# Prompt keys and queries stored once and split in the attention stage

## The chip, the cores and the metric

The kernel runs on one core of one Trainium2 chip. The metric is the device time of one launch in microseconds, the median of three runs. TensorE (PE) multiplies matrices, VectorE (DVE), ScalarE (ACT) and GpSimd (POOL) work on tiles element by element, and SyncE (SP) issues most of the transfers between DRAM and SBUF; PSUM is the memory that PE writes its results to. Times in the profile are counted from the first instruction.

## The reference: what is computed

One inference step of a hybrid decoder with two layers, for a new prompt (1 x 2048 tokens) and, at once, for 8 sequences that each add 8 tokens to 4096 cached ones. D is 1024, with 16 heads of 64.

```python
# layer 1, recurrent (RG-LRU)
z = rms_norm(x) @ w_in; u, g = split(z)
u = causal_conv(u); h = scan(gates(u))
x = x + rms_norm((h * silu(g)) @ w_out)
# keys, values and log forget values, made once
k, v, f = split(rms_norm(x, kv_norm) @ w_kv);  c = cumsum(log_sigmoid(f + b_f))
# layer 2, forgetting attention
q, g = split(rms_norm(x) @ b_w_in)
s = q k^T / 8 + c_query - c_key, causal;  p = softmax(s);  o = p v
y = x + rms_norm((o * silu(g)) @ b_w_out)
```

The outputs are y, the new keys, values and log forget values of prompt and samples, and the recurrent states. Everything is float32. The samples attend to their cached pages, which a page table points to.

## The kernel before, in words

**Precision.** Most products are made in a faster matrix format that keeps fewer bits (F32R). An operand x is split into a high part h, x rounded to that format, and a low part l = x - h, and a product is h·h + h·l + l·h. `evac_pair` (line 361) makes such a pair from PSUM: ACT copies (rounding), DVE subtracts.

**Stages.** The prompt goes through in chunks: the recurrent layer for the first 1024 tokens and the samples, then the projections (`phase_b`, line 859) of keys, values, queries and gates for them; then the recurrent layer for the other 1024, and the projections for these in two chunks of 512 (about 1240 to 1700 us of the profile). `B_ORDER` (line 45) sets the order of the column blocks. In `token_major` (line 885) keys and values come out with a token per partition, go to the outputs, and the values also to a DRAM copy `v_d` (line 915). `keys` (line 871) transposes the keys on PE, splits them with `evac_pair` and writes both parts to `kd_d` (lines 882, 883), which holds a low and a high row for each feature. `feature_major` (line 925) makes queries with a feature per partition, splits them (lines 940, 941) and writes both parts to `qd_d` (lines 943, 944).

**Decode.** `decode` (line 1013) computes attention over the cache for 16 turns (8 sequences, 2 groups of 8 heads). Each turn loads its 32 pages of keys and of values in groups of four (`raw`, line 1074, four buffers), transposes the keys on DVE (line 1159), multiplies on PE (lines 1127 and 1237) and makes a softmax with a block of eight exponentials on ACT (line 1196). Two turns run beside the first projections; the other 14 beside the later projections and the prompt attention.

**Prompt attention** (`attention`, line 1290, about 1700 to 2890 us). A unit is a head and a block of 512 queries; the 64 units run over the heads, 0,1,2,3 and 3,2,1,0 in turn. A head has 40 ticks, one for each block of 128 keys of each of its units. In a tick PE makes the scores `st` (keys by queries) with two matmuls (lines 1537 and 1538), and a third on the diagonal (line 1540) for the mask; ACT makes `p` = exp(st) (line 1546); every four ticks PE multiplies p with the values (`ops`, line 1557); POOL adds up p for the sums (line 106, the helper `tt`). There are two PSUM banks for `st`, so PE can be two ticks ahead of ACT. The row maxima are found first: `top` (line 1394) makes scores `sx` with high parts only (line 1404), DVE reduces them (lines 1406, 1408), and ACT writes the negative maximum into four rows of the query tile (line 1423). `advance` (line 1502) issues these `LEAD` = 18 ticks ahead.

The operands are tiles of 128 rows. `kbt` and `qbt` hold the high part in rows 0 to 63 and, below, the rows for c, the maximum and ones; `ka` holds low and high keys and `qa` high and low queries, so that line 1537 gives both cross products in one pass. `load_keys` (line 1368) fills kbt from the high rows, `load_head` (line 1375) fills ka (both parts) and the values `vvt` from `v_d`, `load_unit` (line 1383) fills qbt and `load_low` (line 1388) qa. A head's keys are loaded at the first tick of the head before, ka and the values three ticks later; a unit's queries one and two units ahead. Before the first unit the loads stand on ACT's queue, then on SP's.

**Order.** The program is written as interleaved generators: `Side.along` (line 1009) runs the decode beside the attention in proportion to estimated costs, and `Later` (line 339) delays steps by ticks. A scheduling pass then sets the order of instructions on each engine, and each engine and each queue works strictly in that order. An SP transfer that waits for a free buffer holds those behind it.

## Time and profile before

| What | Value |
|---|---|
| Median of three runs | 3090.09 us |
| The three runs | 3083.68, 3090.09 and 3090.77 us |
| Span of the profiled execution, first to last instruction | 3081.2 us |
| Time of the profiled execution around its span | not on the page; the median is 8.9 us above the span |
| Granted PE clock, mean of the span | 0.965 |
| Moved by DMA | 653.25 MB, mean 212 GB/s |

How to read it: the page gives the busy time of each engine, and views of the trace give the same for stretches of time (windows), for groups of instructions by line, for waits (who waited for whom: total us, times, longest us), and the chain of waits that leads back from the last instruction. A name like qbt<-qd is what an instruction writes and reads. PEld is PE's loading of weights, SPq and ACTq are transfers issued on those queues. "DMA share" is the mean busy share of the 16 DMA engines and "PEclk" the part of PE's full clock that was granted.

### The profile page before, as it was taken

The page shows a single profiled execution, that of the slowest core. Times are in us where ns is not written, and L with a number is a line of the kernel's source. Part 1 is how long each engine was busy: PE and PEld are TensorE (multiplying, and loading weights), DVE is VectorE, ACT ScalarE, POOL GpSimd, SP SyncE. Part 2 cuts the span into 40 slices and gives each one's busy share as a digit, 9 for nine tenths or more (in the row PEclk, how much of TensorE's full clock was granted, in tenths as well). Part 3 has the DMA queues.
Part 4 walks back from the last instruction along what each step waited for, and adds up shares of the span by engine and source line. Part 5 has one row for each costly group of instructions (what it writes and reads, how often), then busy time and mean ns, then how long its engine had stood idle before and what let it go on. Part 6 is the DMA issues. An engine that isn't in the chain of part 4 may idle for free.

```text
span 3081.2 us, 58151 instructions
## 1 busy us (share of the span) xinstructions
PE 2825.8 (92%) x20462; PEld 2177.5 (71%) x20462; DVE 1805.6 (59%) x4012; ACT 1295.0 (42%) x2874; POOL 1155.5 (38%) x1263
## 2 busy tenths in 40 slices
PE   6998999998999989997999799899999988999798
PEld 5997888988999978885797455455545554544587
DVE  7876555424367756755655666666667665543244
ACT  4665432232346655333333334444444445455211
POOL 1663101000025532000001456655656648788322
PEclk9999999999999999998999799999999999999899
DMA  4224547788622266999999998989999996331343
GB/s 121 89 76 150 154 137 216 242 267 254 198 84 86 79 195 198 327 305 315 325 331 307 292 303 261 289 268 321 289 294 314 317 295 211 97 87 41 96 135 111
DMA packets 492855, 653.25 MB, mean 212 GB/s; under 512 B 91100, under 2 KB 292829, under 8 KB 485286
## 3 DMA queue, kind: packets, MB, share of 16 engines
q1 hardware_dynamic: 488934, 643.87, 66.9%
q10 hardware_dynamic: 3340, 3.56, 0.4%
q8 instruction: 162, 2.65, 0.4%
q0 software_dynamic: 288, 2.10, 0.2%
q14 instruction: 131, 1.07, 0.1%
HBM read 513.82 MB, written 135.16 MB: 211 GB/s over the span
## 4 chain that ended last, share of the span: by engine, by line
PE 54%; DMA 20%; DVE 10%; ACT 5%; SPq 5%; issue 4%; POOL 2%; ACTq 0%; DVEq 0%; POOLq 0%
PE ops L1557 5%; DMA raw<-in_cache_k_dram 5%; PE y L368 4%; PE y L370 4%; PE y L369 4%; PE st L1537 3%; DMA raw<-in_cache_v_dram 3%; PE kv L369 3%; PE kv L368 3%; PE kv L370 3%; PE sx L1404 3%; PE dO L1237 2%; SPq L1074 2%; PE qg L368 2%; PE st L1538 2%
## 5 line engine op out<-in xcount | busy, mean ns | idle before, releaser
L106 POOL TENSOR_TENSOR acc<-acc,p 128x512 f32<-128x512 f32 (+3 forms) x576 | 638.8, 1109 | 291.7 <-PE ops L1557 226.4
L1546 ACT ACTIVATE p<-st 128x512 f32<-128x512 f32 (+3 forms) x576 | 290.4, 525 | 404.8 <-PE st L1538 188.6
L1159 DVE STREAM_TRANSPOSE ktr<-raw 128x1024 f32<-128x1024 f32 x256 | 305.4, 1223 | 161.3 <-DMA raw<-in_cache_k_dram 143.7
L1406 DVE TENSOR_REDUCE mxs<-sx 128x1 f32<-128x512 f32 x384 | 253.9, 680 | 143.5 <-PE sx L1404 142.5
L369 PE MATMUL kv<-wl,xh 128*128 128x256 f32 (+3 forms) x1088 | 309.1, 287 | 8.9 <-DVE wl L413 8.8
L368 PE MATMUL kv<-wh,xh 128*128 128x256 f32 (+3 forms) x1088 | 310.4, 290 | 5.7 <-ACT wh L412 5.3
L370 PE MATMUL kv<-wh,xl 128*128 128x256 f32 (+3 forms) x1088 | 309.2, 286 | 0.0
L1557 PE MATMUL ops<-p,vvt 128*64 128x512 f32 (+3 forms) x1152 | 292.7, 550 | 3.1 <-ACT p L1546 2.8
L1537 PE MATMUL st<-qa,ka 128*128 128x512 f32 (+3 forms) x640 | 273.3, 427 | 21.8 <-ACT p L1546 18.0
L1404 PE MATMUL sx<-kbt,qbt 96*128 96x512 f32 (+3 forms) x640 | 234.7, 426 | 26.1 <-DMA qbt<-qd 11.5
L1537 PEld LDWEIGHTS st<-qa,ka 128*128 128x128 f32 x640 | 123.6, 193 | 178.5 <-issue 112.1
L412 ACT ACTIVATE wh<-wst,gv 128x256 fp32r<-128x256 f32 (+1 forms) x384 | 164.4, 499 | 195.0 <-DMA wst<-in_b_w_in_dram 81.8
L1538 PE MATMUL st<-qbt,kbt 128*128 128x512 f32 (+3 forms) x640 | 237.0, 371 | 0.0
L413 DVE SCALAR_TENSOR_TENSOR wl<-wst,gv,wh 128x256 fp32r<-128x256 f32 (+1 forms) x384 | 169.9, 492 | 108.1 <-ACT wh L412 100.3
L368 PE MATMUL qg<-xh,wh 128*128 128x384 f32 (+2 forms) x640 | 229.1, 359 | 1.0 <-ACT wh L412 1.0
L370 PE MATMUL qg<-xh,wl 128*128 128x384 f32 (+2 forms) x640 | 227.5, 357 | 0.9 <-DVE wl L413 0.9
L369 PE MATMUL qg<-xl,wh 128*128 128x512 f32 (+2 forms) x640 | 226.9, 356 | 0.0
L1092 POOL TENSOR_TENSOR qw<-qb,amask 128x128 f32<-128x128 f32 x64 | 29.3, 465 | 498.8 <-PE dS L1127 258.0
L369 PEld LDWEIGHTS kv<-wl,xh 128*128 128x128 f32 (+1 forms) x1088 | 203.8, 188 | 12.7 <-DVE wl L413 10.4
L368 PEld LDWEIGHTS kv<-wh,xh 128*128 128x128 f32 (+1 forms) x1088 | 203.6, 189 | 11.8 <-ACT wh L412 6.0
L370 PEld LDWEIGHTS kv<-wh,xl 128*128 128x128 f32 (+1 forms) x1088 | 205.3, 189 | 3.9 <-issue 3.9
L1404 PEld LDWEIGHTS sx<-kbt,qbt 96*128 96x128 f32 x640 | 119.1, 203 | 94.4 <-DVE mxs L1406 25.1
(289 smaller groups left out, 6472.1 us busy)
## 6 DMA issues: line engine op xcount, KB each, us to landing
raw<-in_cache_k_dram SPq DMA_DIRECT2D x512, 256.0 KB
raw<-in_cache_v_dram SPq DMA_DIRECT2D x512, 256.0 KB
wst<-in_w_kv_dram SPq DMA_DIRECT2D x48, 512.0 KB
wst<-in_b_w_in_dram SPq DMA_DIRECT2D x48, 512.0 KB
xt<-in_x_prompt_dram SPq DMA_DIRECT2D x32, 512.0 KB
wst<-in_a_w_in_dram SPq DMA_DIRECT2D x64, 256.0 KB
x<-x SPq DMA_DIRECT2D x32, 512.0 KB
out_dram<-kf SPq DMA_DIRECT2D x128, 128.0 KB
```

The source lines that it names most:

```text
L106: eng.tensor_tensor(out, a, b, op=op)
L368: T.matmul(ps, lh(k), rh(k), start=(k == 0), stop=False)
L369: T.matmul(ps, lh(k), rl(k), start=False, stop=False)
L370: T.matmul(ps, ll(k), rh(k), start=False, stop=(k == nk - 1))
L413: V.scalar_tensor_tensor(wl[:, k, :], st[:, k, :], gk, f(wh[:, k, :]), op0=ALU.mult, op1=ALU.subtract)
L1159: V.transpose(t.kts[pp][:, n], raw[:, :, pp * 256:(pp + 1) * 256])
L1404: T.matmul(ps[:, :w], qb[0:96, j * P:(j + 1) * P], kb[0:96, ck * 512:ck * 512 + w], start=True, stop=True)
L1406: V.reduce_max(mx[:, j, ck:ck + 1], ps[:, :w], axis=AX.X)
L1537: T.matmul(ps[:, lo:], ka[:, ks], qa[:, lo:], start=True, stop=False)
L1538: T.matmul(ps[:, lo:], kb[:, ks], qb[:, lo:], start=False, stop=(k < qc * 4))
L1546: pair.append((k, lo, p, A.activation(p[:, lo:], ps[:, lo:], AF.Exp)))
L1557: return T.matmul(ops[r:r + HD, lo:], vvs[h % 2][:, k, :], p[:, lo:], start=(k < 2), stop=(last and k >= todo[-1][0] - 1))
```

## The change

`kd_d` and `qd_d` hold each key and query once, in float32. In the projections, ACT copies keys and queries from PSUM to one tile, which is written; DVE's subtractions there and the second writes go. The DRAM copy of the values goes too; the attention reads values from the output.

In the attention, a head's keys are loaded once, into rows 0 to 63 of ka. `split_keys` then makes both parts for each of four chunks of 512 keys, at ticks 10 to 13 of the head before: ACT copies with rounding into kbt and into rows 64 to 127 of ka, and DVE subtracts in place for the low part. A unit's queries are loaded once, into rows 0 to 63 of qa; `split_unit` copies on ACT to qbt, subtracts on DVE into rows 64 to 127, and copies in place on ACT to round. Loads are issued one unit earlier than before (`bring`), and a unit is split five ticks after its load, or when it is needed (`part`). qa has six buffers in place of four. To make room, tiles of the recurrent layer move to a pool that is closed before the attention, and the tiles `cs` and `odd` share one buffer.

```diff
-    kd_d, qd_d = dt_("kd", [D, 2, SEQ]), dt_("qd", [D, 2, SEQ])
+    kd_d, qd_d = dt_("kd", [D, SEQ]), dt_("qd", [D, SEQ])
-    v_d = dt_("vd", [SEQ, D])
...
-                evac_pair(th[:, :w], tl[:, :w], ps[:, :w])
+                A.copy(tf[:, :w], ps[:, :w])
-                S.dma_start(kd_d[r0:r0 + P, 1, tk:tk + w], f(th[:, :w]))
-                S.dma_start(kd_d[r0:r0 + P, 0, tk:tk + w], f(tl[:, :w]))
+                S.dma_start(kd_d[r0:r0 + P, tk:tk + w], tf[:, :w])
...
-                        S.dma_start(v_d[tok:tok + m, sl], kf[:m, :])
...
-                            A.mul(th[:, :nn], ps[:, :nn], 0.125)
-                            V.scalar_tensor_tensor(tl[:, :nn], ps[:, :nn], 0.125, f(th[:, :nn]),
-                                                   op0=ALU.mult, op1=ALU.subtract)
-                            S.dma_start(qd_d[r * P:(r + 1) * P, 0, pt:pt + w], f(th[:, so:nn]))
-                            S.dma_start(qd_d[r * P:(r + 1) * P, 1, pt:pt + w], f(tl[:, so:nn]))
+                            A.mul(tf[:, :nn], ps[:, :nn], 0.125)
+                            S.dma_start(qd_d[r * P:(r + 1) * P, pt:pt + w], tf[:, so:nn])
...
         def load_keys(h):
-                queue[0].dma_start(f(kb[0:64, lo:hi]), kd_d[h * HD:(h + 1) * HD, 1, lo:hi])
+                queue[0].dma_start(f(ka[0:64, lo:hi]), kd_d[h * HD:(h + 1) * HD, lo:hi])
                 queue[0].dma_start(f(kb[64:67, lo:hi]), nc_d[h, :, lo:hi])
+        def split_keys(h, c):
+            ka, kb = heads[h], kbs[h % 2]
+            sl = slice(c * 512, (c + 1) * 512)
+            A.copy(kb[0:64, sl], f(ka[0:64, sl]))
+            A.copy(ka[64:P, sl], f(ka[0:64, sl]))
+            tt(V, ka[0:64, sl], f(ka[0:64, sl]), f(kb[0:64, sl]), ALU.subtract)
+            loaded.add((h, c))
...
-            queue[0].dma_start(f(qbs[u % NQ][0:64, :]), qd_d[h * HD:(h + 1) * HD, 0, qc * 512:(qc + 1) * 512])
-        def load_low(u):
...
+            qa = qas[u] = pool.tile([P, 512], F32R, name="qa", tag="qa", bufs=NQ)
+            queue[0].dma_start(f(qa[0:64, :]), qd_d[h * HD:(h + 1) * HD, qc * 512:(qc + 1) * 512])
+        def split_unit(u):
+            qa, qb = qas[u], qbs[u % NQ]
+            A.copy(qb[0:64, :], f(qa[0:64, :]))
+            tt(V, qa[64:P, :], f(qa[0:64, :]), f(qb[0:64, :]), ALU.subtract)
+            A.copy(qa[0:64, :], f(qa[0:64, :]))
...
+        def bring(u, tick):
+            while done[1] <= min(u, len(units) - 1):
+                load_unit(done[1])
+                since[done[1]] = tick
+                done[1] += 1
...
+            if done[0] < len(tasks):
+                bring(min(tasks[done[0]][0] + 2, done[2] + NQ - 1), tick)
+            if done[3] < done[1] and since[done[3]] + 5 <= tick:
+                part(done[3])
...
+                if 10 <= at < 14 and h + 1 < H:
+                    split_keys(h + 1, at - 10)
```

More of the change, by code (lines that the diff above doesn't have):

```diff
@@ L221, in tile_hawk_fox, with kt_ @@
     small = ctx.enter_context(tc.tile_pool(name="small", bufs=4))
+    wkeep = ExitStack()
+    wkept = sbuf(wkeep, "slots")
+    def kt_(name, shape):
+        return wkept.tile(shape, F32, name=name, tag=name)
+    gv = kt_("gv", [P, KB, 43])
+    hb_ga, hb_gx = kt_("hb_ga", [P, KB]), kt_("hb_gx", [P, KB])
+    nsp4, psp4 = kt_("nsp4", [P, KB]), kt_("psp4", [P, KB])
+    bfB = kt_("bfB", [P, H])
+    halo = kt_("halo", [P, KB, 3])
+    G.memset(halo[:, :, :], 0.0)
+    hcar = kt_("hcar", [P, KB])
+    G.memset(hcar[:, :], 0.0)
+    ccar = kt_("ccar", [H, 1])
+    G.memset(ccar[:, :], 0.0)
+    st_s = kt_("st_s", [P, KB, 32])
+    st_p = kt_("st_p", [P, KB, 4])
     def rsqrt(ss, m, scale, post=None, w=1):
@@ L1317, in attention @@
         pool.tile([P, 512], F32, name="oT", tag="oT", bufs=5)
-        pool.tile([P, 512], F32, name="cs", tag="cs")
+        pool.tile([P, 512], F32, name="odd", tag="odd")
         pool.tile([P, 512], F32, name="sgt", tag="sgt", bufs=2)
@@ L1460, in total @@
                 T.matmul(ps[qc * 32:(qc + 1) * 32, :], ones[:, :32], acc[:, :], start=True, stop=True)
-            cs = pool.tile([P, 512], F32, name="cs", tag="cs")
+            cs = pool.tile([P, 512], F32, name="cs", tag="odd")
             rows = slice(0, P) if len(todo) == 4 else slice(qc * 32, (qc + 1) * 32)
@@ L1499, in attention, with part @@
         start = [sum(nks[:u]) for u in range(len(units))]
-        done = [0, 0, 0]
+        done = [0, 0, 0, 0]
+        since = {}
+        def bring(u, tick):
[3 more added lines that the diff above has]
+                done[1] += 1
+        def part(u):
+            while done[3] <= u:
+                split_unit(done[3])
+                done[3] += 1
         def advance(tick):
@@ L1510, in advance @@
                 u, j, ck = tasks[done[0]]
-                while done[1] <= min(u + 1, len(units) - 1):
-                    load_unit(done[1])
-                    done[1] += 1
+                bring(u + 1, tick)
+                part(u)
                 top(u, j, ck)
                 done[0] += 1
+            if done[0] < len(tasks):
+                bring(min(tasks[done[0]][0] + 2, done[2] + NQ - 1), tick)
+            if done[3] < done[1] and since[done[3]] + 5 <= tick:
+                part(done[3])
         load_keys(0)
         tick = 0
+        split_keys(0, 0)
+        split_keys(0, 1)
         advance(-1)
-        load_head(0)
-        load_low(0)
-        load_low(1)
+        load_values(0)
+        split_keys(0, 2)
+        split_keys(0, 3)
         queue[0] = S
```

46 lines of the change are left out of this document (11 added, 35 removed).

## The prediction

> **What bounds the kernel now.** The page first: it has the span, and which engine is near its limit.
>
> ```profile
> span 3081.2 us, 58151 instructions
> PE 2825.8 (92%) x20462; PEld 2177.5 (71%) x20462; DVE 1805.6 (59%) x4012; ACT 1295.0 (42%) x2874; POOL 1155.5 (38%) x1263
> ```
>
> TensorE (PE) is busy 92% of the span. An average over stages says little, so the second view is the windows over the stretches that the change touches: the second pass of the projections (1240 to 1700 us), the start of the prompt attention, the attention with the decode beside it, the attention alone, and, for comparison, the projections' first pass.
>
> ```profile
> core 0: us, PE busy (x) PEld busy (x) DVE busy (x) ACT busy (x) POOL busy (x), PEclk, DMA share, GB/s
> 1240.00:1700.00 460.00, 430.07 (x3936) 368.47 (x3938) 271.06 (x524) 159.15 (x409) 20.09 (x35) 0.96 0.98 319
> 1700.00:1740.00 40.00, 23.12 (x148) 14.02 (x140) 21.20 (x49) 6.60 (x17) 11.28 (x17) 0.61 1.04 303
> 1740.00:2560.00 820.00, 751.09 (x6624) 427.81 (x6622) 554.24 (x1131) 360.75 (x877) 507.76 (x490) 0.96 0.94 294
> 2560.00:2890.00 330.00, 300.47 (x1346) 158.04 (x1342) 149.55 (x346) 169.94 (x358) 259.36 (x227) 0.98 0.34 93
> ...
> 400.00:870.00 470.00, 448.39 (x3805) 431.82 (x3806) 211.49 (x442) 137.04 (x349) 16.87 (x44) 0.99 0.71 220
> ```
>
> Here the DMA engines are as full as PE: 0.98 and 0.94 of the time from 1240 to 2560 us. PE is idle 460 - 430.07 = 29.9 us in the projections, 820 - 751.09 = 68.9 us beside the decode, 29.5 us in the attention alone. The third view is the chain of waits, for the projections and for the attention beside the decode:
>
> ```profile
> by line: DMA raw<-in_cache_k_dram 12.7%; PE kv L369 7.4%; PE kv L368 7.3%; PE kv L370 7.2%; DMA wst<-in_w_kv_dram 6.2%; DMA sgd<-tgb 5.7%; DMA sc<-cd 4.7%; SPq L1074 4.5%; issue 3.8%; PE dS L1127 3.6%; DVE wl L413 3.6%; PE qg L368 3.5%; DMA
> by line: PE ops L1557 11.3%; DMA raw<-in_cache_k_dram 10.2%; DMA raw<-in_cache_v_dram 8.5%; PE st L1537 7.4%; PE dO L1237 6.6%; PE sx L1404 6.3%; SPq L1074 5.6%; PE dS L1127 5.1%; issue 4.9%; PE st L1538 4.9%; DMA sc<-cd 4.8%; DVE ktr L1159
> ```
>
> Transfers alone are 12.7 + 6.2 + 5.7 + 4.7 = 29.3% of the first chain and 10.2 + 8.5 + 4.8 = 23.5% of the second. The fourth view, the waits in 1740 to 2560 us, tells what PE stood still for, and what VectorE (DVE) did:
>
> ```profile
> PE dO L1237 <- DMA raw<-in_cache_v_dram: 21.9, 14, 5.1
> PE dS L1142 <- DVE sc L106: 8.3, 4, 4.1
> PE st L1537 <- ACT p L1546: 7.6, 16, 1.6
> PE sx L1404 <- DVE mxs L1406: 5.6, 9, 1.3
> PE dm L1179 <- DVE dmx L1177: 3.4, 1, 3.4
> PE dS L1127 <- DVE ktr L1159: 3.4, 2, 1.7
> ```
> ```profile
> DVE ktr L1159 <- DMA raw<-in_cache_k_dram: 62.2, 33, 4.6
> ```
>
> Cache pages hold PE directly for 21.9 us, and hold DVE for 62.2 us, behind which the row maxima of the prompt queue up. DVE holds PE for 8.3 + 5.6 + 3.4 + 3.4 = 20.7 us. So this stretch is bound by PE and the transfers together, with DVE third.
>
> **The change, part by part: transfers removed.**
>
> ```profile
> qa<-qd SPq DMA_DIRECT2D x62, 256.0 KB
> ka<-kd SPq DMA_DIRECT2D x15, 1024.0 KB
> ...
> kd<-ktl SPq DMA_DIRECT2D x32, 256.0 KB
> vd<-kf SPq DMA_DIRECT2D x64, 128.0 KB
> ...
> qbt<-qd SPq DMA_DIRECT2D x61, 128.0 KB
> kbt<-kd SPq DMA_DIRECT2D x15, 512.0 KB
> ...
> qd<-qtl SPq DMA_DIRECT2D x16, 256.0 KB
> ```
>
> A head's keys came in 1024 + 512 KB and will come in 512; its four query units in 4 x (256 + 128) and will come in 4 x 128. That is 2048 KB, 2.1 MB, less for each of 16 heads. A head lasts (2890 - 1740) / 16 = 72 us, so 11.4 heads lie in the 820 us: 23.9 MB of 294 x 820 = 241 MB, 9.9%. The projections no longer write the low halves of keys and queries or the copy of the values; half of the 2048 tokens fall in 1240 to 1700 us: 16 x 256 KB, as much for the queries, and 32 x 128 KB, 12.6 MB of 319 x 460 = 147 MB, 8.6%. The other half falls before 870 us, where the DMA share is 0.71 and PE is busy 448 of 470 us; nothing is counted there (bounds: nothing and those 22 us). The values of a head come as before, from the output in place of the copy, with the same runs of 64 floats: nothing.
>
> What is a tenth of a full resource worth? At least nothing (what remains can be the decode's own latency), at most all idle time of PE in the two stretches, 98.8 us, and its clock: granted 0.96, so up to 4% of 430 + 751 busy us, 47 us. [...] I take half of the idle time, 15 + 34 us, and a fifth of the clock, 9 us: **-58 us**.
>
> **Work added to ScalarE (ACT) and DVE.** The rows for a copy or subtraction of 512 columns:
>
> ```profile
> L1438 ACT COPY oT<-ops 64x512 f32<-64x512 f32 x64 | 37.1, 579 | 107.0 <-PE ops L1557 107.0
> ...
> L941 DVE SCALAR_TENSOR_TENSOR qtl<-qg,qth 128x384 fp32r<-128x384 f32 (+2 forms) x40 | 23.2, 587 | 19.0 <-DMA qd<-qtl 8.9 <-ACT qth L940 7.7 <-DMA kd<-ktl 2.4
> L106 DVE TENSOR_TENSOR ktl<-kt,kth 128x512 fp32r<-128x512 f32 x32 | 21.6, 683 | 54.7 <-ACT kth L99 49.3 <-DMA kd<-ktl 5.4
> ```
>
> In the projections 72 DVE subtractions go, 21.6 + 23.2 = 44.8 us. DVE is at 271 of 460 us there and no row of it leads the chain: nothing. In the attention, keys take two copies and a subtraction for each of 4 chunks of 16 heads, queries the same for each of 64 units: 256 ACT copies x 0.579 = 148 us and 128 subtractions.
>
> ACT: 11.4 heads x 16 copies x 0.579 = 106 us raise it beside the decode from 361 to 467 of 820 us. ACT works in order, so an exponential (p, which PE needs to free a score bank) waits behind the copies. The order of the changed program has the eight copies of a head's keys mostly in one block. The nearest thing in the trace is the eight exponentials of a decode softmax, also in one block on ACT; these windows are ten such blocks:
>
> ```profile
> 1763.90:1768.10 4.20, 3.29 (x16) 1.33 (x12) 3.38 (x9) 4.20 (x19) 3.96 (x4) 1.00 0.97 332
> ...
> 2521.50:2526.00 4.50, 2.66 (x13) 1.38 (x9) 4.50 (x12) 4.50 (x18) 2.87 (x4) 1.00 0.55 161
> sum 46.80, PE 38.53 PEld 19.02 DVE 44.14 ACT 46.55 POOL 32.46; mean PE 3.85 PEld 1.90 DVE 4.41 ACT 4.65 POOL 3.25
> ```
>
> PE idles 46.80 - 38.53 = 8.3 us in them, against 8.4% of 46.80, 3.9 us, at the stretch's usual rate: 4.4 us for 46.6 us of ACT, 0.094 us each. So 148 us cost **+14 us**; bounds nothing (the gaps of ACT are as wide as its work) and 50.
>
> DVE: one subtraction is 0.683 us from a PSUM operand. The new ones read two SBUF operands while GpSimd (POOL) adds, also from SBUF. The nearest rows are subtractions of twice the width from SBUF, the first beside those additions, the second after them:
>
> ```profile
> L106 DVE TENSOR_TENSOR wol<-wst,woh 128x1024 fp32r<-128x1024 f32 x8 | 13.3, 1660 | 5.8 <-ACT woh L99 5.8
> ```
> ```profile
> L106 DVE TENSOR_TENSOR olT<-ogT,ohT 128x1024 fp32r<-128x1024 f32 x14 | 17.2, 1225 | 81.0 <-ACT ohT L99 81.0
> ```
>
> 1660 against 1225 ns: 1.36 times as long. 0.683 x 1.36 = 0.93 us, times 128 = 119 us, of which 8 x 11.4 x 0.93 = 85 us beside the decode: DVE goes from 554 to 639 of 820 us, 68% to 78%. PE's 20.7 us of waits for DVE grow; as the measure I take DVE's busy time over its idle time, 68/32 = 2.1 now and 78/22 = 3.5 then, two thirds more: **+14 us**. Bounds: nothing, if DVE only fills the 62.2 us in which it waits for pages, and 85, all of it in PE's path. POOL, 259 of 330 us busy in the attention alone, loses as it waits in turn: **+3 us** (nothing to 4.6 heads x 8 x 0.68 = 25).
>
> The Trainium skill, SBUF — State Buffer, section Who interferes with whom, speaks against this change at this place: a VectorE instruction with two SBUF inputs and a GpSimd instruction that reads SBUF exclude each other for the whole instruction. By that rule the trace's 1660 against 1225 ns is such a wait, and a subtraction that always met the start of a POOL addition would cost a whole addition; the sum goes by the 0.93 us.
>
> **The start of the attention.** Now the query loads are issued while the keys are still coming:
>
> ```profile
> 1713.47 2.39 PE L1404 MATMUL sx<-kbt,qbt 96*128 96x128 f32 x6 [11.55 <-DMA qbt<-qd]
> ```
> ```profile
> 1705.55 2.02 ACTq L1386 DMA_DIRECT2D qbt<-qd  x3
> ```
>
> In the changed order of ACT's queue, five query loads stand behind four copies that wait for the first keys, and 29 copies (both first heads, six units) stand ahead of the first exponential: 29 x 0.579 = 17 us. Against that, ka (1024 KB) no longer follows. I take **+8 us**, bounds nothing and 25.
>
> The buffer shared by odd and cs makes one copy wait for a small transfer, once in eight units, with at least two ticks between: nothing; uncovered, by the mean wait for a page, 21.9 / 14 = 1.6 us, 13 us at eight places.
>
> **Sum**: -58 + 14 + 14 + 3 + 8 = **-19 us**, on a span of 3081.2: 3062. The page gives no time around the span; the median shown, 3090.09, is 8.9 us above it, and I carry that over: **3071 us**.
>
> **Rivals.**
> - DVE takes the place of the transfers (slower). For it: 78% on an engine that works in order, shares its operand path with POOL, and carries the decode's transposes; the cache waits fall on DVE, not on PE. If half of its 119 us lands in PE's path (60) and the relief is half of mine (29), with 25 for ACT, POOL and the start: 3090 + 60 - 29 + 25 = 3146 at worst, and 3090 + 40 - 40 + 25 = 3115 if a third of it does and the relief is 40. It decides once DVE is above about 80% beside the decode. Against it: DVE, 68% busy today, holds PE for only 20.7 of 820 us.
> - The splits wait for their loads (slower). A unit is split five ticks, about 9 us, after its load is issued; one load above took from 1705.55 to 1713.47. If one in four of 64 units holds ACT, and so PE, for 3 us: 48 - 19, 3119 us. Against it: PE's rows above name no query load as late, and the traffic ahead of a load shrinks.
> - The transfers were the bound, fully. By the bytes, 12.6 MB at 319 GB/s and 23.9 MB at 294 are 39 + 81 us; PE's idle time caps the gain at 99, and with the 39 us of costs that gives 3090 - 99 + 39 = 3030.
> - It washes out: the cache waits come from the decode's order and not from the load, relief 40, costs 39: 3091.
>
> **How the numbers follow.** Chances: forecast 0.34, transfers fully 0.12, wash 0.16, DVE 0.27, late splits 0.11. The range leaves out the ends of the first and the worst of the DVE case: 3020 to 3140; faster cases alone, 3020 to 3080. A measurement of this kernel tells about 0.3%, 9 us, from no change; Of the forecast 0.30 lies below that bound and 0.04 within it; of the wash 0.02 below, 0.12 within, 0.02 above. Faster 0.44, same 0.16, slower 0.40.
>
> **What would show it.** The DMA share beside the decode falls to about 0.86 and PE's waits for raw below 15 us (relief); PE's waits for mxs, sc and ktr under 45 us and the subtractions near 0.9 us (DVE); p waits for copies little (ACT); the first st at most 10 us later after the last gate projection. I am wrong if the DMA share stays above 0.92 with less traffic, if ACT's waits name DMA qa or ka, or if DVE passes 80%.

## The result and the profile after

The changed kernel takes 3169.1 us (median of four runs, 3162.65 to 3170.41) against 3088.0 us for the kernel before on the same chip: a ratio of 1.0266, with an interval of 1.0251 to 1.0282. It is slower by 2.7%; the forecast was 3071 us, faster, and the time lies above the range of 3020 to 3140 too.

The page of the changed kernel, span and engines:

```profile
span 3160.9 us, 58116 instructions
PE 2864.8 (91%) x20462; PEld 2185.8 (69%) x20462; DVE 1866.2 (59%) x4068; ACT 1439.9 (46%) x3130; POOL 1170.8 (37%) x1263
```

PE has the same 20462 matmuls as before, and yet 2864.8 - 2825.8 = 39.0 us more busy time; its idle time, span less busy, goes from 255.4 to 296.1 us, 40.7 more. So half of the 79.7 us is PE standing still, and half is PE running slower. Where? The source view of the second matmul of the scores (first and last start of its 640, before and after), and of the last gate projection, mark the stages:

```profile
L1538 PE MATMUL st<-qbt,kbt x640: 271/389/736, 1731.0 to 2882.4; 128*128 128x512 f32 x160
```
```profile
L1562 PE MATMUL st<-qbt,kbt x640: 226/389/773, 1719.1 to 2965.4; 128*128 128x512 f32 x160
```
```profile
L375 PE MATMUL qg<-xh,wl x640: 302/338/503, 428.3 to 1673.7; 128*128 128x384 f32 x64, 128*128 128x512 f32 x64, 128*128 128x320 f32 x32
```

The attention starts 11.9 us earlier, and its last scores come 83 us later. Windows, cut at the first score, the decode's last page matmul and the last product with the values; first the kernel before, then the changed one, with the projections ahead:

```profile
1731.00:2572.40 841.40, 772.49 (x6761) 439.42 (x6759) 565.03 (x1154) 370.20 (x897) 521.49 (x502) 0.96 0.94 294
2572.40:2885.40 313.00, 287.67 (x1259) 152.12 (x1252) 140.35 (x326) 163.93 (x345) 244.25 (x213) 0.98 0.32 87
```
```profile
1240.00:1680.00 440.00, 421.35 (x3945) 362.33 (x3943) 249.93 (x486) 154.32 (x398) 13.13 (x27) 0.97 0.93 301
1719.10:2543.70 824.60, 725.03 (x6389) 406.67 (x6389) 588.02 (x1157) 417.10 (x966) 469.13 (x445) 0.93 0.83 262
2543.70:2968.40 424.70, 374.04 (x1557) 192.13 (x1550) 206.48 (x439) 247.29 (x508) 308.98 (x269) 0.95 0.19 54
```

The attention took 841.4 + 313.0 = 1154.4 us and takes 824.6 + 424.7 = 1249.3, 94.9 more. PE's busy time in it grows by 725.03 + 374.04 - 772.49 - 287.67 = 38.9 us and its idle time by 56.0. The transfers did fall as forecast: DMA share 0.94 to 0.83. The granted clock fell as well, 0.96 to 0.93 and 0.98 to 0.95. What PE waited for in the attention (us, times, longest), before (beside the 21.9 us for pages that are shown above) and after:

```profile
PE st L1537 <- ACT p L1546: 18.0, 33, 2.9
...
PE sx L1404 <- DVE mxs L1406: 6.7, 11, 1.3
PE ops L1557 <- ACT p L1546: 6.5, 11, 1.5
```
```profile
PE st L1561 <- ACT p L1570: 45.2, 50, 5.2
PE ops L1581 <- ACT p L1570: 22.5, 20, 5.9
PE sx L1407 <- DVE mxs L1411: 14.3, 14, 2.9
PE sx L1407 <- DVE mxs L1409: 13.1, 20, 2.1
PE dO L1233 <- DMA raw<-in_cache_v_dram: 12.1, 10, 3.2
```

The cache pages hold PE for 9.8 us less; the exponentials hold it for 45.2 + 22.5 - 18.0 - 6.5 = 43.2 us more. And ACT, which makes the exponentials, waits itself, at the new copies (lines 1375, 1393 and 1395):

```profile
ACT qbt L1393 <- DMA qa<-qd: 54.0, 29, 6.5
...
ACT kbt L1375 <- DMA ka<-kd: 21.5, 12, 3.7
...
ACT qa L1395 <- DVE qa L106: 19.7, 21, 1.9
```

The timeline of SP, ACT and PE shows one head's key copies, with the issue of their load first (start, duration; in brackets idle time before, and what ended it):

```profile
2150.07 0.49 SPq L1368 DMA_DIRECT2D ka<-kd  x1
...
2159.51 0.62 ACT L1375 CAST kbt<-ka 64x512 fp32r<-64x512 f32 x1 [2.11 <-DMA ka<-kd]
...
2159.99 0.40 PE L1562 MATMUL st<-qbt,kbt 128*128 128x512 f32 x1
...
2160.14 0.62 ACT L1376 CAST ka<-ka 64x512 fp32r<-64x512 f32 x1
...
2163.95 0.62 ACT L1376 CAST ka<-ka 64x512 fp32r<-64x512 f32 x1
2164.59 0.62 ACT L1393 CAST qbt<-qa 64x512 fp32r<-64x512 f32 x1
2165.12 1.06 ACT L1570 ACTIVATE p<-st 128x512 f32<-128x512 f32 x2
...
2165.76 0.80 PE L1561 MATMUL st<-qa,ka 128*128 128x512 f32 x1 [5.24 <-ACT p L1570]
...
2166.35 0.63 PE L1562 MATMUL st<-qbt,kbt 128*128 128x512 f32 x1
```

ACT waits 2.11 us for the keys, makes eight copies and one more, and only then the exponential that PE has waited for, 5.24 us. The matmul after the wait takes 0.63 us where the one before took 0.40. Windows of 3.4 us over the same place show why (PE busy is the second number, the granted clock the third from the end):

```profile
2158.50:2161.90 3.40, 2.01 (x11) 1.25 (x7) 3.40 (x6) 2.35 (x4) 3.24 (x3) 1.00 0.77 183
2161.90:2165.30 3.40, 0.00 (x0) 0.00 (x0) 3.29 (x6) 3.30 (x7) 2.29 (x2) 0.91 0.78 233
2165.30:2168.70 3.40, 2.94 (x9) 1.60 (x13) 3.34 (x8) 3.40 (x13) 2.78 (x2) 0.50 1.01 371
2168.70:2172.10 3.40, 3.40 (x27) 0.96 (x21) 2.74 (x9) 3.38 (x13) 1.28 (x2) 0.59 0.20 75
2172.10:2175.50 3.40, 3.40 (x14) 1.14 (x15) 2.71 (x6) 2.08 (x6) 1.35 (x2) 1.00 0.82 176
```

A wait is paid twice: 5.24 us idle, and then some 6 us at half clock, which is 3 us more. The traces' record of the clock has only the values 1.0 and 0.5, so the means of the attention's windows are 2 x (0.04 x 841.4 + 0.02 x 313.0) = 80 us at half clock before and 2 x (0.07 x 824.6 + 0.05 x 424.7) = 158 us after: 78 us more, worth 39 us, which is about the growth of PE's busy time. The means are rounded to hundredths; the record itself gives 85.6 and 162.3 us, 76.7 more.

### The profile page after: what moved, and what is told of

Its sections match the earlier page's. It is cut to its first block, busy times and chain, and to the rows that moved or that the text cites. A ratio compares the mean times of both kernels' runs of the same rounds, so it can differ in the third digit from the quotient of the medians.

```text
span 3160.9 us, 58116 instructions
## 1 busy us (share of the span) xinstructions
PE 2864.8 (91%) x20462; PEld 2185.8 (69%) x20462; DVE 1866.2 (59%) x4068; ACT 1439.9 (46%) x3130; POOL 1170.8 (37%) x1263
## 4 chain that ended last, share of the span: by engine, by line
PE 51%; DMA 14%; ACT 6%; DVE 6%; issue 4%; SPq 3%; POOL 2%; DVEq 0%; ACTq 0%; POOLq 0%
PE ops L1581 7%; PE st L1561 4%; DMA raw<-in_cache_k_dram 3%; PE sx L1407 3%; PE kv L373 3%; PE kv L374 3%; PE kv L375 3%; PE y L375 3%; PE y L373 3%; PE y L374 3%; PE dS L1123 3%; PE dO L1233 3%; PE qg L373 2%; PE qg L374 2%; PE st L1562 2%
## 5 line engine op out<-in xcount | busy, mean ns | idle before, releaser
L106 POOL TENSOR_TENSOR acc<-acc,p 128x512 f32<-128x512 f32 (+3 forms) x576 | 646.7, 1123 | 280.0 <-PE ops L1581 201.9
L1561 PE MATMUL st<-qa,ka 128*128 128x512 f32 (+3 forms) x640 | 279.0, 437 | 52.2 <-ACT p L1570 45.2
L1581 PE MATMUL ops<-p,vvt 128*64 128x512 f32 (+3 forms) x1152 | 311.0, 573 | 4.6 <-ACT p L1570 4.5
L375 PE MATMUL qg<-xh,wl 128*128 128x512 f32 (+2 forms) x640 | 226.6, 354 | 0.3 <-DVE wl L417 0.3
```

What stands on the lines that cost most here:

```text
L106: eng.tensor_tensor(out, a, b, op=op)
L375: T.matmul(ps, ll(k), rh(k), start=False, stop=(k == nk - 1))
L1561: T.matmul(ps[:, lo:], ka[:, ks], qa[:, lo:], start=True, stop=False)
L1581: return T.matmul(ops[r:r + HD, lo:], vvs[h % 2][:, k, :], p[:, lo:], start=(k < 2), stop=(last and k >= todo[-1][0] - 1))
```

## The experiments

Theory A is that the splits, on ACT's in-order queue, hold up the exponentials. The rivals: B, the subtractions on DVE; C, the order of the decode, which the scheduling pass draws forward in the changed kernel (its last page matmul stands at score tick 387 of 640, before at 439); D, that fewer transfers are worth nothing. All ratios are to runs of the kernel before on the same chip in the same session. PE busy is from each page, PE idle the span less that; both are of one profiled execution, which can lie some 12 us off the run's median.

| Run | Ratio, interval | PE busy, idle (us) |
|---|---|---|
| before | 1 | 2825.8, 255.4 |
| changed | 1.0266 (1.0251 to 1.0282) | 2864.8, 296.1 |
| no splits | 0.9980 (0.9954 to 1.0005) | 2822.9, 250.4 |
| copies only | 1.0142 (1.0108 to 1.0176) | 2852.4, 265.9 |
| subtractions only | 1.0152 (1.0130 to 1.0175) | 2864.3, 263.8 |
| splits later | 1.0295 (1.0271 to 1.0318) | 2859.8, 291.8 |
| before, decode early | 1.0073 (1.0048 to 1.0097) | 2834.5, 266.6 |
| no splits, decode late | 0.9965 (0.9948 to 0.9983) | 2836.1, 240.4 |
| changed, decode late | 1.0236 (1.0200 to 1.0273) | 2857.2, 283.9 |
| keys and queries spread | 1.0008 (0.9987 to 1.0029) | 2841.3, 247.6 |
| keys spread | 1.0130 (1.0100 to 1.0159) | 2854.8, 281.0 |
| queries spread | 1.0153 (1.0117 to 1.0190) | 2857.5, 285.1 |
| before, copies in blocks | 1.0103 (1.0068 to 1.0138) | 2849.2, 266.2 |
| before, copies one by one | 1.0142 (1.0114 to 1.0169) | 2841.6, 282.5 |
| before, tiny copies | 1.0032 (1.0011 to 1.0052) | 2841.9, 265.4 |
| spread one by one, decode late | 1.0122 (1.0099 to 1.0145) | 2857.6, 268.1 |
| spread, decode late | 1.0136 (1.0099 to 1.0174) | 2861.2, 275.3 |
| spread one by one | 1.0048 (1.0024 to 1.0073) | 2840.3, 268.1 |
| before, half the loads | 0.9994 (0.9978 to 1.0010) | 2830.2, 251.6 |
| before, values from output | 1.0045 (1.0029 to 1.0062) | 2831.2, 252.1 |

### What do the splits cost?

**No splits.** ka and qa become fixed tiles, and the splits are made only while these are filled for the first time:

```diff
+            if h < 2:
                 A.copy(kb[0:64, sl], f(ka[0:64, sl]))
                 A.copy(ka[64:P, sl], f(ka[0:64, sl]))
                 tt(V, ka[0:64, sl], f(ka[0:64, sl]), f(kb[0:64, sl]), ALU.subtract)
...
+            if u < NQ:
                 A.copy(qb[0:64, :], f(qa[0:64, :]))
                 tt(V, qa[64:P, :], f(qa[0:64, :]), f(qb[0:64, :]), ALU.subtract)
                 A.copy(qa[0:64, :], f(qa[0:64, :]))
```

> The changed kernel, with the splits made only for the first two heads and the first six units; after that the tiles keep the old rounded parts beside the new loads, so the attention's result is not the reference's. All transfers, matmuls and buffers are those of the changed kernel, and the decode's last page matmul stands at score tick 381 of 640 (387 in the changed kernel, 439 before). Theory A (the splits, on ACT's in-order queue, hold up the exponentials): nearly the whole loss goes and the relief of the transfers is left alone, 3030 to 3060 us. Rival B (the subtractions on DVE): the same here, told apart by the next two runs. Rival C (what costs is that the decode is drawn forward, which leaves more of the attention without it): 3120 to 3150 us, since the order stays. Rival D (the relief of the transfers beside the decode is about nothing): near the 19 us of the projections alone, 3065 to 3085 us.

Measured 0.9980. The splits cost 1.0266 - 0.9980 = 2.9%, 88 us: theory A or B, not C. And what is left is no relief of 30 us or more, but 6 us, hardly told from nothing, as D has it. The stage beside the decode:

```profile
1721.20:2488.90 767.70, 695.58 (x6273) 396.17 (x6275) 528.85 (x1076) 328.99 (x814) 449.13 (x434) 0.95 0.89 281
```

**Copies only**, the same conditions around the subtractions alone (`if h < 2` and `if u < NQ` ahead of the two `tt` lines):

> The changed kernel without the subtractions on DVE after the first two heads and six units (the low parts stay stale, so the attention's result is not the reference's); all copies on ACT are kept, but the copy in place no longer waits for a subtraction. Theory A: the copies and their waits for loads are left, so most of the loss stays, 3130 to 3160 us. Rival B: 3050 to 3080 us. Rival C: within 10 us of the changed kernel, 3160 to 3175 us.

**Subtractions only**, the conditions around the three copies alone (the stale high parts and the new differences still add up to the same keys and queries):

> The changed kernel without the copies on ACT after the first two heads and six units (stale high parts, so the attention's result is not the reference's); DVE makes all its subtractions, from the stale parts. Theory A: 3040 to 3080 us, since ACT's stream is the old one and DVE gives 128 times 0.8 us beside other work. Rival B: 3130 to 3165 us. Rival C: within 10 us of the changed kernel.

Measured 1.0142 and 1.0152 (3118 and 3127 us), both between the ranges of A and B. Neither A nor B alone: put on the run without splits, the copies cost 1.62%, 50 us, and the subtractions 1.72%, 53 us; together they cost 88, so part of it is shared. The second sum has something that the changed kernel has not: with no copy ahead of them, DVE's subtractions wait for the loads themselves.

```profile
DVE qax L106 <- DMA qax<-qd: 22.6, 19, 5.3
...
DVE kax L106 <- DMA kax<-kd: 11.3, 7, 3.4
```

**Splits later.**

```diff
-            if done[3] < done[1] and since[done[3]] + 5 <= tick:
+            if done[3] < done[1] and since[done[3]] + 9 <= tick:
...
-                if 10 <= at < 14 and h + 1 < H:
-                    split_keys(h + 1, at - 10)
+                t0 = 10 if h % 2 == 0 else 16
+                if t0 <= at < t0 + 4 and h + 1 < H:
+                    split_keys(h + 1, at - t0)
```

> The changed kernel with the splits later: queries nine ticks after their load in place of five, and the keys of every second head at ticks 16 to 19 in place of 10 to 13. The work is the same, but the loads have more time, so that ACT's waits for qa and ka (58 us beside the decode) should mostly go. Theory A in the form that ACT's waits for loads are the greater part: 3125 to 3150 us. In the form that the copies' own time in the queue is the greater part: 3160 to 3175 us. Rivals B and C: 3160 to 3175 us.

Measured 1.0295, and the wait at line 1393 is as it was, 53.5 us in place of 54.0. It tells nothing of the theories: the scheduling pass puts the copies where it did before, whatever the tick. In both traces each copy into kbt and qbt stands behind the same number of exponentials, a head's first key copy 0 to 5 exponentials into the head before, although the source has it at tick 10 or later. The source says when a copy may stand, the pass says where.

### Is it the order of the decode?

One constant, the decode's share: `SHARE = 1.30` in the kernel before, `SHARE = 0.80` without splits and in the changed kernel (1.13 in both as they are).

> The kernel before with one constant changed: the decode's share of the order raised from 1.13 to 1.30, so that its last page matmul stands at score tick 384 of 640, as in the changed kernel (387), in place of 439. Rival C (drawing the decode forward costs by itself): 3095 to 3120 us, since 55 ticks more are left without the decode, while the transfers set the decode's pace. If the order costs nothing: within 0.3% of the kernel before.

> The run without the splits, with the decode's share lowered from 1.13 to 0.80, so that its last page matmul stands at score tick 427 (381 without this, 439 before). It leaves out the same splits, so the attention's result is not the reference's. Rival C: the relief that the run without splits did not show comes out, 3035 to 3060 us. Rival D (fewer transfers beside the decode are worth about nothing): within 0.3% of the run without splits, 3065 to 3085 us.

> The changed kernel with the decode's share lowered from 1.13 to 0.80, so that its last page matmul stands at score tick 435 (387 without this). All of the work stays. Rival C: 3130 to 3155 us. If the order costs nothing: 3155 to 3175 us. It also says whether the changed kernel was only badly balanced: if that were so, under 3088 us.

Measured 1.0073, 0.9965 and 1.0236 (3106, 3074 and 3151 us). The first and the last lie in the ranges given for C, but C falls for the attention. With the decode early, the attention of the kernel before takes 2905.6 - 1751.7 = 1153.9 us, against 1154.4; the loss is ahead of it. The share holds for the projections too: the last gate projection starts 1698.9 - 1692.9 = 6.0 us later, and the first score 1751.7 - 1731.0 = 20.7 us later. The other two differ from their partners (0.9980, 1.0266) by less than the intervals can tell.

### Is it where the copies stand on ACT?

**Keys and queries spread.** Each chunk's and each unit's splits are queued behind the exponential of their own tick:

```diff
+                exp = A.activation(p[:, lo:], ps[:, lo:], AF.Exp)
...
+                with tc.issue_after(exp.ins):
+                    if 10 <= at < 14 and h + 1 < H:
+                        split_keys(h + 1, at - 10)
+                    if done[3] < done[1] and since[done[3]] + 5 <= tick:
+                        part(done[3])
                 before = done[0]
                 advance(tick)
```

> The changed kernel with each chunk's copies, and each unit's, queued on ACT behind the exponential of their own tick. In the changed kernel the scheduling pass puts the eight copies of a head's keys next to each other, 8 times 0.617 = 4.9 us without an exponential; here two copies stand between exponentials. The work, the loads and the ticks are the same. Theory A in the form that the blocks of copies starve PE (and half its clock for some us after): 3115 to 3145 us. If the copies' sum counts, however they stand: 3155 to 3170 us. Rival B (the subtractions): 3155 to 3170 us.

Measured 1.0008: better than either expectation. All the work is there, 256 copies and 128 subtractions, and the loss is gone. ACT's waits for the loads of qa and ka are gone with the blocks (from the first score on, the list has only the wait for DVE's subtraction), and PE's waits for p are nearly those of before:

```profile
ACT qa L1395 <- DVE qa L106: 32.0, 31, 3.5
```
```profile
PE st L1557 <- ACT p L1566: 21.8, 42, 2.0
...
PE ops L1578 <- ACT p L1566: 7.6, 14, 1.5
```

The edit does two things at once. It breaks the blocks up, and it moves the copies away from their loads: in the changed kernel a head's first key copy starts 7.3 us after the issue of its load (mean of 15 heads), with both spread 25.9 us; a unit's first query copy 5.5 and 20.6 us (mean of the 58 units after the first six).

**Keys alone, queries alone**, with one of the two conditions in the block above, the other left where it was:

> The changed kernel with the keys' chunks alone queued behind the exponentials of their ticks; the queries' copies stand where the scheduling pass puts them, and still wait for their loads (54 us of ACT in the changed kernel). If the blocks of eight copies are the greater part of the loss: 3095 to 3120 us. If the queries' waits for their loads are: 3135 to 3160 us.

> The changed kernel with the queries' copies alone queued behind the exponentials of their ticks, five ticks after the load; the keys' copies stay in blocks of eight. It is the missing corner beside the changed kernel (1.027), keys alone (1.013) and both (1.001). If the two costs stand side by side: 1.012 to 1.018 of the kernel before, 3120 to 3140 us. If the blocks of the keys are no cost in themselves, as the copies added to the kernel before suggest, and the queries' waits for their loads are all: under 1.007, 3085 to 3105 us.

Measured 1.0130, between the two ranges, and 1.0153, as forecast for two costs side by side. With the changed kernel (1.0266) and both (1.0008) that is a table of two by two, and the two costs add: spreading the keys is worth 1.36% with the queries left and 1.45% with them spread, spreading the queries 1.13% and 1.22%. What ACT still waits for, with the keys spread and with the queries spread:

```profile
ACT qbt L1393 <- DMA qa<-qd: 92.2, 43, 10.8
```
```profile
ACT kbt L1375 <- DMA ka<-kd: 20.1, 9, 9.3
```

Each run keeps the wait of the half that it leaves.

**Blocks without the rest.** In the kernel before, eight copies for each of 15 heads, of the next head's ka onto itself; in a block, one by one, or one by one and tiny:

```diff
+                if at == 20 and h + 1 < H:
+                    with tc.issue_after(exp.ins):
+                        for i in range(8):
+                            same = heads[h + 1][i % 2 * 64:i % 2 * 64 + 64, i // 2 * 512:i // 2 * 512 + 512]
+                            A.copy(same, f(same))
```
```diff
-                if at == 20 and h + 1 < H:
+                if 20 <= at < 28 and h + 1 < H:
...
-                        for i in range(8):
+                        i = at - 20
```
```diff
-                        same = heads[h + 1][i % 2 * 64:i % 2 * 64 + 64, i // 2 * 512:i // 2 * 512 + 512]
+                        same = heads[h + 1][i % 2 * 64:i % 2 * 64 + 64, i // 2 * 512:i // 2 * 512 + 4]
```

> The kernel before, with eight copies of 64x512 added on ACT for each of 15 heads, next to each other behind the exponential of tick 20. They copy the next head's ka onto itself, long after its load, and nothing of the result changes. They are the changed kernel's key copies without the loads, the subtractions and the new order: 120 times 0.617 = 74 us of ACT. Block theory: 15 stalls of about 4 us on PE, and some us at half clock after each, 3125 to 3150 us. If only the sum of the copies counts: 3090 to 3105 us, as in the run with them one by one.

> The same 120 copies in the kernel before, one behind the exponential of each of the ticks 20 to 27. Block theory: the two st banks cover 0.6 us, so within 0.4% of the kernel before, 3085 to 3098 us. If the sum counts: the same time as the run with blocks.

> The kernel before with 120 copies of 64x4 in place of 64x512, one behind the exponential of each of the ticks 20 to 27: ACT has almost none of the 74 us of work, but the scheduling pass is given the same added instructions. If the work is what cost 1.4% with the long copies: within 0.4% of the kernel before, 3080 to 3097 us. If it is the changed order (any change of it costs about 1%): 3110 to 3130 us.

Measured 1.0103, 1.0142 and 1.0032. The first (3117 us) lies between its two ranges, the second (3128 us) far above the block theory's. That theory falls in this form: a block whose data are long there is no dearer than single copies. Beside the block of eight that starts at 2160.12 us and takes 5.01 us, PE has products with the values, scores and products of the decode, and does not stand still; that the pass reckons with the block's length and puts them there is an inference. PE's longest wait for p is 1.7 us with blocks (the first line) and 3.8 with single copies (the second), where the changed kernel had 5.2:

```profile
PE st L1537 <- ACT p L1546: 15.8, 25, 1.7
```
```profile
PE st L1537 <- ACT p L1546: 24.2, 36, 3.8
```

But the same copies are not cheap either. Their groups, long and tiny:

```profile
L1576 ACT CAST ka<-ka 64x512 fp32r<-64x512 f32 x120 | 73.9, 616 | 1.2
```
```profile
L1576 ACT CAST ka<-ka 64x4 fp32r<-64x4 f32 x120 | 22.8, 190 | 2.4
```

One by one, 73.9 - 22.8 = 51.1 us of ACT cost 1.0142 - 1.0032 = 1.1%, 34 us, about two thirds of themselves; the new instructions and the order that shifts with them cost 0.3%, at the bound of what can be told.

**A better version?** The spread kernel with the decode late (`SHARE = 0.88`), the keys' copies one to a tick with the share as it was, and both:

```diff
-                    if 10 <= at < 14 and h + 1 < H:
-                        split_keys(h + 1, at - 10)
+                    if 6 <= at < 14 and h + 1 < H:
+                        split_keys(h + 1, (at - 6) // 2, (at % 2,))
+                    while rest:
+                        round_unit()
```

> The changed kernel with all of its work, in the order that the runs so far suggest: the keys' copies one to a tick (ticks 6 to 13), the queries' copy in place one tick after the other copy, each behind its tick's exponential, and the decode's share 0.88, so that its last page matmul stands at tick 399. By the run without splits (0.9965 to 0.998 of the kernel before) little is to be won: 3065 to 3085 us, 0.2 to 0.6% faster than the kernel before, if nothing but the blocks and waits was wrong; within 0.3% of it if the subtractions and the sum of the copies keep what they cost with two copies together.

> The run with both spread, with the decode's share 0.88 in place of 1.13, so that its last page matmul stands at tick 412 (381 without this). It was one of two changes of the run with copies one by one, which came out 1.2% slower than the kernel before. If the share is what cost there: 3115 to 3130 us. If the order of the decode costs nothing, as in the runs without splits: within 0.5% of the kernel before, 3075 to 3100 us.

> The run with copies one by one, with the decode's share back at 1.13, so that only the spacing of the copies (one to a tick, from tick 6) differs from the run with both spread. If the spacing is what cost: 3115 to 3130 us. If the share was: within 0.5% of the kernel before, 3080 to 3100 us.

Measured: both edits 1.0122, the decode late alone 1.0136, one copy to a tick alone 1.0048. The share is what cost, although it cost nothing without splits. ACT's waits for the loads of qa are small in all three (5.1, 10.9 and 0.2 us), and its waits for DVE's subtraction do not follow the loss (23.2, 61.9 and 36.9 us; 32.0 with both spread at the old share), so neither explains it. A part lies at the start: from the last gate projection to the first score the run with the decode late takes 1699.9 - 1647.6 = 52.3 us and the one with both spread 1719.2 - 1681.9 = 37.3, 15.0 of the 47.6 us between their spans. In the attention PE also has more time at half clock, 160 us by the clock's record against 104 (a granted 0.93 beside the decode with the share at 0.88, 0.94 with it at 1.13):

```profile
1699.90:2570.10 870.20, 777.09 (x6822) 436.74 (x6825) 642.40 (x1227) 443.18 (x1030) 504.20 (x466) 0.93 0.85 265
```
```profile
1719.20:2493.10 773.90, 710.96 (x6417) 402.28 (x6419) 598.05 (x1159) 416.54 (x972) 465.84 (x437) 0.94 0.89 284
```

No version with the splits beats the kernel before; the best is level with it.

### Where did the relief go?

**Half the loads** in the kernel before: ka and qa fixed tiles, loaded for the first two heads and the first four units only.

```diff
-            for lo, hi in halves(h):
+            for lo, hi in halves(h) if h < 2 else ():
                 queue[0].dma_start(f(ka[:, lo:hi]), kd_d[h * HD:(h + 1) * HD, :, lo:hi].rearrange("d x t -> (d x) t"))
...
+                if u < 4:
                     queue[0].dma_start(f(qa[:, :]), qd_d[h * HD:(h + 1) * HD, :, qc * 512:(qc + 1) * 512].rearrange("d x t -> (d x) t"))
```

> The kernel before with the loads of ka left out after the first two heads and those of qa after the first four units (the tiles keep old data, so the attention's result is not the reference's). That takes away 14 times 1.05 MB and 60 times 0.26 MB, 30 MB, what the change takes from the attention's loads, and nothing is split; the decode's last page matmul stands at tick 424 (439 before). By the prediction's term for these loads (34 us of waits and 9 us of clock): 3040 to 3055 us. If the transfers beside the decode are worth nothing, as the runs without splits say: within 0.4% of the kernel before, 3075 to 3095 us.

**Values from the output**, alone:

```diff
-    v_d = dt_("vd", [SEQ, D])
-                    else:
-                        S.dma_start(v_d[tok:tok + m, sl], kf[:m, :])
-            queue[0].dma_start(vvs[h % 2][:, :, :], v_d[:, hr].rearrange("(k p) d -> p k d", p=P))
+            queue[0].dma_start(vvs[h % 2][:, :, :], vp_flat[:, hr].rearrange("(k p) d -> p k d", p=P))
```

> The kernel before with the values read from the output, and without their DRAM copy: 8.4 MB of writes less in the projections, and the rest as it was. By the prediction's term for the projections (15 us for 25 MB): about 5 us, 3080 to 3088 us. If the writes of the projections are worth what the earlier start of the attention in the changed kernel says (12 us for 25 MB): 4 us. A loss of more than 0.3% would be one of order.

Measured 0.9994 and 1.0045. Thirty MB less in the attention, and no gain: D is shown there. The windows and the waits say how. The DMA share beside the decode falls from 0.94 to 0.88, and PE waits for the cache's pages not less but more, 33.3 us in place of 21.9:

```profile
1724.30:2549.30 825.00, 752.35 (x6692) 427.05 (x6692) 550.76 (x1129) 357.81 (x876) 499.98 (x484) 0.96 0.88 273
2549.30:2884.60 335.30, 308.97 (x1341) 161.16 (x1334) 150.42 (x350) 173.65 (x366) 265.79 (x231) 0.98 0.22 59
```
```profile
PE dO L1237 <- DMA raw<-in_cache_v_dram: 33.3, 19, 3.6
```

That wait was not for a share of a full resource. The stage beside the decode is shorter by 841.4 - 825.0 = 16.4 us, with the decode ending at tick 424 in place of 439; the attention alone is longer by 335.3 - 313.0 = 22.3. The values' edit is a loss of 0.45%, against an expected gain of about 5 us. Its profiled execution was the fastest of its ten and within 2.1 us of the one before (3083.3 us), so the loss has no place in a trace; but the trace shows where a gain goes. The attention starts 1731.0 - 1709.8 = 21.2 us earlier, with the same part of the decode done (708 of the 2112 dO matmuls), and then takes 2886.2 - 1709.8 = 1176.4 us, 22.0 longer, of which 859.7 - 841.4 = 18.3 beside the decode:

```profile
1709.80:2569.50 859.70, 779.27 (x6735) 441.31 (x6735) 557.25 (x1148) 366.12 (x892) 513.31 (x496) 0.94 0.92 290
```

Why it takes longer there is open.

## Why the prediction was wrong

**Transfers removed, -58 us: failed; about -6.** The step that failed is "What is a tenth of a full resource worth?", where half of PE's idle time was put down to the load of the DMA engines. In the attention 30 MB less are worth 0.06% (an interval of -0.10% to 0.22%), against 43 us in the sum. No run shows that half: with the share at 0.88 in place of 0.94, PE's waits for the pages of values rose from 21.9 to 33.3 us. The test that the prediction set, a share of about 0.86 and waits for raw below 15 us, came out as forecast (0.83 and 12.1 us), and would have been read as a hit; the waits moved without the time. The rival "It washes out: the cache waits come from the decode's order and not from the load" had this half right. In the projections the forecast 15 us look about right at their end: it comes 1692.9 - 1673.7 = 19.2 us earlier, of which 11.9 are left at the first scores. But that is partly luck. The values' edit alone, a third of these bytes, brings the last gate projection 1692.9 - 1672.3 = 20.6 us forward, and nothing of it is left at the end; and DVE's subtractions, which went too, were not tried alone.

**Work added to ACT and DVE, +14 and +14: failed; +88 together.** The copies' number and duration were right (617 against 579 ns), and the subtractions' nearly (0.91 us for queries and 0.73 for keys, 104 us in all, against 0.93 and 119):

```profile
L1393 ACT CAST qbt<-qa 64x512 fp32r<-64x512 f32 x64 | 39.2, 617 | 54.4 <-DMA qa<-qd 54.0
L106 DVE TENSOR_TENSOR qa<-qa,qbt 64x512 fp32r<-64x512 f32 x64 | 58.2, 912 | 53.8 <-ACT qbt L1393 52.5
L106 DVE TENSOR_TENSOR ka<-ka,kbt 64x512 fp32r<-64x512 f32 x64 | 46.0, 727 | 22.6 <-ACT ka L1376 22.4
```

The price of 0.094 us for each us on ACT was the step that failed. It came from the decode's eight exponentials, at which the windows show ACT busy for 46.55 of 46.80 us; the new copies wait for loads (54.0 and 21.5 us), with the exponentials behind them, and PE waits 43.2 us more for p. The copies alone, put on the run without splits, cost the upper bound that was given (without a working) for them, 50 us, and the subtractions 53, inside theirs of 85: the values taken near the lower ends were wrong, not the bounds. The condition named for being wrong, that ACT's waits name DMA qa or ka, is what the trace shows, 54.0 and 21.5 us. The rival "The splits wait for their loads" had the waits, a chance of 0.11, and with 64 / 4 x 3 = 48 us about half of the price of 88: it counted the queries alone and no clock. The DVE rival's point did not come: DVE is at 588.02 / 824.6 = 71%, under the 80 from which it was to decide, and yet the subtractions alone cost 53 us in their own run.

**The clock was counted on the wrong side.** It was to rise by a fifth of its loss, 9 us; it fell, by 39 us. The forecast put no price on a wait beyond its length. So even right waits would have given a sum too small.

**Start of the attention, +8: held.** From the last gate projection to the first st 1719.1 - 1673.7 = 45.4 us, before 1731.0 - 1692.9 = 38.1: 7.3 later. **POOL, +3:** 778.11 - 765.75 = 12.4 us more busy time in the attention, within its bounds; what that cost was not tried alone.

**What is shown and what is not.** Shown: the loss is the splits', 88 us; the same splits cost next to nothing in another order on ACT, and keys and queries share the gain about evenly; 30 MB less in the attention are worth nothing here. Argued only: that the waits for late loads, and not the blocks, are the part that the spreading removes. For it stand the waits that go with the loss, the longer way from load to copy (7.3 and 25.9 us for keys), the blocks with data there, which are no dearer than single copies, and the run with the keys spread, which has no blocks of eight left, waits for the queries' loads and loses 1.3%; against it that the sums of the waits do not follow the loss (92.2 us with the keys spread at 1.3%, 20.1 with the queries spread at 1.5%). No run has the splits in blocks with their loads long there. Open: why the decode's share is worth 1.3% with the splits spread and nothing without them, beyond the 15.0 us at the start, and why the time that the projections win is lost in the attention.

## What to carry to other kernels

Added work on an engine that works in order is priced by what stands behind it in its queue and by whether its data are there; the same 256 copies and 128 subtractions cost 0.3% here (1.0008 less 0.9980) or 2.9% (1.0266 less 0.9980), by place alone, so look at the order that the scheduling pass makes and pin it before the work is judged. A resource that is 94% busy need not be a bound: take bytes away in a run of its own before you count on them. Time won in one stage can be lost in the next, so judge by the end of the kernel and not by the start of a stage. Where the matrix engine's clock falls after a pause, price a wait of some microseconds at more than its length: here 40.7 us more idle time came with 39.0 us of slower matmuls.

## What the runs showed of the hardware

- Cut into stretches of 3.41 us, the attention of the kernel before has 5 in which PE is busy for less than 40%, of 339, and the changed one 14 of 365; 18 of these 19 are followed by one at under 0.75 of the clock. Of those with PE busy over 90%, 8 of 511 are. Only three of the 19 are empty, so it need not be a whole idle stretch. In the clock's record of the two runs, 79 of 81 periods at half clock last 3.41 us or a multiple of it. The Trainium skill, TensorE: Matmul & The Clock Gate, Part 1, says that a free-running window of 3413 ns decides and that an idle one halves the clock; the trace agrees with the length, and the empty stretch above, 2161.90 to 2165.30 us, followed by one at 0.50, is such a case. That partly busy stretches did it too is what these traces show beyond that.
- A copy of 64x4 on ACT takes 190 ns, one of 64x512 takes 616: 508 more columns add 426 ns, so nearly all of the small copy's time is not its columns.
- The subtractions of 64x512 take 912 ns on the mean for qa and 727 ns for ka, but their medians are nearly alike, 686 and 680 ns. In the changed kernel's trace the 75 that overlap no GpSimd tensor instruction take no more than 687 ns; the 53 that do take 1058 ns (qa, 39 of 64) and 907 ns (ka, 14 of 64) on the mean, and up to 1797 ns.
